# One block of a transformer on one core: the lower part of every fourth piece of split weights is made by ScalarE and an adding DMA instead of VectorE

## The chip, the core and the metric

The kernel runs on one core of a Trainium2 chip. The core has TensorE (PE, matrix products), VectorE (DVE), ScalarE (ACT), GpSimd (POOL) and SyncE (SP), an on-chip memory of 128 partitions, PSUM banks in which products add up, and 16 DMA engines that all queues share. The metric is the device time of one execution in microseconds (us), the median of the runs shown.

## What is computed

A block for 256 tokens of width 2048: a feed-forward part, a mixing part (eight heads of retention and eight of sparse attention, whose 64 keys for each query are chosen by an index score), and a second feed-forward part, each behind a norm and added to x, then a last norm. All in float32.

```python
x = x + 0.5 * swiglu(rmsnorm(x, ffn1_norm[l]), ffn1_w_gate[l], ffn1_w_up[l], ffn1_w_down[l])
h = rmsnorm(x, mix_norm[l])
proj = h @ w_in[l]
...
x = x + jnp.concatenate([ro, ao], axis=-1) @ w_out[l]
x = x + 0.5 * swiglu(rmsnorm(x, ffn2_norm[l]), ffn2_w_gate[l], ffn2_w_up[l], ffn2_w_down[l])
return rmsnorm(x, final_norm)
```

Nearly all of the work is in the products with the weights: gate and up (2048 x 5632 each) and down (5632 x 2048), twice, w_in (2048 x 6480) and w_out (2048 x 2048).

## The kernel before

**Products in two parts.** TensorE takes float32r, a float32 with fewer bits. To keep the accuracy, each weight W is split into hi, the rounded W, and lo = W - hi, and the activations likewise. A product is hi times both parts of the activations (512 columns: 256 tokens of each part, line 137) plus lo times the upper part (256 columns, lines 136 and 139). Where tokens stand still and the weights move (the values, lines 154 to 156) there are three products.

**Pieces and loads.** The weights are a stream of 686 pieces, counted here from 0. A usual piece is four k tiles (128 rows of a weight each) by 256 columns, 128 x 1024 numbers on chip. A load brings two pieces, 1 MB, into a tile raw of which there are three. A chunk of 256 columns of gate, up or a projection has four pieces; a chunk of a down projection has six, the last of them half as wide. A step of the program is the work beside the products of one piece: before the products of piece i, `split` is written for piece i+4, and other work (evacuation, silu, rotation, scores, softmax, retention) is put at fixed steps by `after`.

**Splitting.** `split` (line 204) first issues loads on SP's queue until two more than the piece's own are under way. A load waits for its raw tile, that is for the splits of the two pieces that lay there. Then ACT makes hi by a copy that rounds, and DVE makes lo by a subtraction. hi and lo have five buffers each (BUFS), so piece i+5 can be split when the products of piece i are done.

**Order.** Each engine runs its instructions in the order in which the program writes them; a semaphore is waited for where one reads or overwrites what another made. POOL has little to do: four masks of the scores (`causal`, line 603), and the loads of the constants, the positions (line 412), decay and qdec (lines 676 and 678, `ret_consts`), the last two needed by the retention (`ret_s`, line 700).

Of the kernel before, what the change touches and what calls it, by code (L numbers as in the profile page):

```python
# [19 lines left out]
P = 128  # L20
T = 256          # tokens
D = 2048         # model width
KT = D // P      # 16
FF = 5632
NCH = FF // 256  # 22 chunks of 256 hidden columns
HCH = NCH // 2   # 11 chunks in each half
HKT = 2 * HCH    # 22 k tiles in each half
NH = 8           # retention heads, attention heads
NI = 16          # index heads
TOPK = 64  # L30
EPS = 1e-6
FIRST_SQ = 4     # the step of the first squares of x
BUFS = 5         # split pieces of weights on chip
NEG = -3.0e38    # marks a score that is out or already taken
BIG = -1.0e30    # added to the logits of keys that are not attended
W_AV = 256 + NI
C_TWO_PI = 2.0 * math.pi
C1 = 6.28125                       # 2 pi in parts whose products with n < 2**16 are exact
C2 = round((C_TWO_PI - C1) * 2**17) / 2**17
# [6 lines left out]
def layer(ctx: ExitStack, tc: tile.TileContext, a: dict, out: bass.AP):  # L46
# [23 lines left out]

# [1 line left out]
    gains = new(one, [P, 4 * KT + NH], F32, "gains")  # L72
# [3 lines left out]

# [1 line left out]
    loads = []   # lists of (offset, source)  # L78
    pieces = []  # dict(load, off, n, mm); a step is the work beside one piece's products
    raws, split_of = {}, {}  # L80
    ends = {}    # step -> functions

    def after(step, fn):
        ends.setdefault(step, []).append(fn)

    # a function may be a generator of stages; it yields the steps from one stage to the next
    chains = []
# [13 lines left out]
    class Chunk:  # L101
        """Where the products of a chunk of columns add up: a bank for each block of 128."""
        acc = None
# [9 lines left out]
    class LastChunk:  # L113
        """The same, with the first block complete before the last piece's products for the second"""

# [7 lines left out]
    def mm_cols(chunk, blocks, kts, rhs, first, last):  # L123
        """W[k, 128 cols] stationary; the split activations [k, hi | lo] move."""

        def go(hi, lo):
            order = [(i, b) for i in range(len(kts)) for b in range(blocks)]
            if last and isinstance(chunk, LastChunk):
                order.sort(key=lambda ib: ib[1])
            for i, b in order:  # L130
                acc = chunk.bank(b)
                r = rhs(kts[i])
                st, sp = first and i == 0, last and i == len(kts) - 1
                c = (i * blocks + b) * P
                if sp:
                    TE.matmul(acc[:, T:], lhsT=lo[:, c:c + P], rhs=r[:, :T], start=False, stop=False)  # L136
                TE.matmul(acc, lhsT=hi[:, c:c + P], rhs=r, start=st, stop=sp)  # L137
                if not sp:
                    TE.matmul(acc[:, T:], lhsT=lo[:, c:c + P], rhs=r[:, :T], start=False, stop=False)  # L139

        return go

    def mm_rows(chunk, n, kts, rhs, first, last):
        """Tokens stationary; W[k, n cols] moves."""

# [14 lines left out]
    def block(src, l0, l1, width):  # L160
        """k tiles l0 to l1 of a chunk, which lie in DRAM as one block"""
        return src[P * l0 * width:P * l1 * width].rearrange("(p n) -> p n", p=P)

    def stream(src, kts, width, per_load, per_piece, rhs, chunk, maker, arg):
        """One chunk of columns over all its k tiles."""
        n = len(kts)
        for l0 in range(0, n, per_load):
            l1 = min(n, l0 + per_load)
            loads.append([(0, block(src, l0, l1, width))])
            for k0 in range(l0, l1, per_piece):  # L170
                k1 = min(l1, k0 + per_piece)
                pieces.append(dict(load=len(loads) - 1, off=(k0 - l0) * width, n=(k1 - k0) * width,
                                   mm=maker(chunk, arg, kts[k0:k1], rhs, k0 == 0, k1 == n)))
        return len(pieces)   # the step after the chunk's last

    def stream_pair(srcs, rhs, chunks):
        """The first two chunks side by side, while x is loaded."""
        for k0 in range(0, KT, 4):
# [25 lines left out]
    def split(i):  # L204
# [9 lines left out]
        S.activation(hi[:, :p["n"]], raw, AF.Copy)  # L214
        V.tensor_tensor(lo[:, :p["n"]], raw, hi[:, :p["n"]].bitcast(F32), op=OP.subtract)  # L215
        split_of[i] = (hi, lo)

# [1 line left out]
    s2 = {}  # L219

    def split_x(c, norm):
        """x * gain of two k tiles, split, for the next projections."""
        t = new(one, [P, 2, 512], F32R, f"xg{c}")
# [19 lines left out]
    def rsqrt(o, v, n):  # L243
        """o = v ** -0.5"""
        q = new(tmp, [P, 2 * NH], F32, "rs_q", 1)[:, :n]
# [6 lines left out]
    def act_table(fn):  # L252
        """An early use of fn, for the table that a later one needs."""
        t = new(tmp, [P, 1], F32, "table", 1)
# [4 lines left out]
    def row_of(tok):  # L259
        """[tokens, 2] -> [128, tokens], the same row in each partition, in PSUM"""  # L260
        diag = new(tmp, [P, 2, P], F32, "diag", 1)
# [8 lines left out]
    def add_squares(ps, sq, first, last):  # L270
        """Sums over the partitions of sq, a column for each token tile, in a bank of its own"""
        for t in range(2):
# [22 lines left out]

# [1 line left out]
    def ffn(which, norm, next_norm, last):  # L297
# [76 lines left out]
    def finish(chunk):  # L374
        """The last two k tiles of x, and the final norm."""
        c = KT // 2 - 1
# [15 lines left out]

# [1 line left out]
    nc.scalar.dma_start(gains, a["gains"])  # L394
# [11 lines left out]

    # cos and sin: [cos, sin] of the 128 wide heads, then of the index heads
    rot = new(one, [P, 4, T], F32, "rot")

    def tables():  # L410
# [23 lines left out]
        yield 1  # L434
        # what the rounding of n left outside of [-pi, pi]
        V.tensor_scalar(n, ang, 1.0 / C_TWO_PI, MAGIC, op0=OP.mult, op1=OP.add)
# [12 lines left out]

    # ================= the program =================  # L450
    def first_squares():
# [8 lines left out]

# [1 line left out]
    m0 = len(pieces)  # L462
# [8 lines left out]

    heads = {}   # name -> tiles of four blocks [128, 4, 256]
    done_at = {}
# [39 lines left out]
    cols("iq", a["w_iq"], 4, True)  # L513
    # index keys, in both halves of the partitions
    ikT = new(one, [P, 1, T], F32, "ikT")
    chunk_ik = Chunk()
    end = stream(a["w_ik"], list(range(KT)), 128, 16, 8, rhs_x, chunk_ik, mm_cols, 1)
    after(end, lambda: rope(chunk_ik, 1, ikT, True))
    # attention values and index weights, by token
    avw = new(one, [P, 2, W_AV], F32, "avw")  # L520
# [50 lines left out]

    # -- index scores, one query tile each --
    score = [new(one, [P, P], F32, "score0"), new(one, [P, T], F32, "score1")]

    def index_scores(t, h0, n):
        """n heads from h0 of query tile t: score += w * relu(q . k). Heads of the two halves of
        the partitions take different row tiles of the array, and different banks."""
        w = P if t == 0 else T
# [36 lines left out]
    def bias(t):  # L615
        """0 where a key was taken, BIG elsewhere"""
        V.tensor_scalar(score[t], score[t], NEG, BIG, op0=OP.not_equal, op1=OP.mult)
        causal(score[t], t, BIG)

# [50 lines left out]

    # -- retention --
    ret = {}
# [86 lines left out]

    # when  # L760
    s = m_av + 1
# [18 lines left out]
    for i in range(2):  # L780
        after(s + i, lambda i=i: k_tok(4 * i))
    for g in range(2):   # heads 0-3, 4-7
        h0 = 4 * g
# [33 lines left out]

# [1 line left out]
    n = len(pieces)  # L819
    n_split = 0  # L820
    for i in range(n):
        # the first pieces wait for their loads: work that is ready should not queue behind them
        ahead = 2 if i < 11 else BUFS - 1
# [11 lines left out]
def _constants():  # L835
    f = np.float32
    lg = np.log1p(-np.exp2(-5.0 - np.arange(NH, dtype=np.float64)))
    j = np.arange(P, dtype=np.float64)
    diff = j[None, :] - j[:, None]                                   # [key j, query i]
    decay = np.where(diff >= 0, np.exp(np.maximum(diff, 0.0)[:, None, :] * lg[None, :, None]).transpose(1, 0, 2),  # L840
                     0.0).transpose(1, 0, 2) * 128.0 ** -0.5          # [key j, head, query i]
    qdec = np.exp((j + 1)[None, :] * lg[:, None])                    # [head, query i]
    kdec = np.exp((P - 1 - j)[:, None] * lg[None, :]) * 128.0 ** -0.5
# [10 lines left out]
def _tiles(w, cols, per_load=8):  # L854
    """[k, n] -> [chunk of cols, k * cols]: what one load brings is one block [128, k tile * cols]"""
    k, n = w.shape
# [45 lines left out]
```

## Time and profile before

| what | value |
| --- | --- |
| median of 2 runs | 1932.65 us (1932.54 to 1932.77) |
| the profiled execution, from the first to the last instruction | 1931.7 us |
| busy: PE, DVE, ACT, POOL | 1914.8, 1207.8, 924.9, 5.3 us |
| moved by DMA | 356.44 MB |
| share of the 16 DMA engines taken by the weights' queue | 53.5% |

The profiled execution's own time is its span of 1931.7 us; the timed median lies 0.95 us above. Busy time is the time in which an engine runs an instruction; waiting and issuing DMAs are not in it. The chain is the series of instructions and waits that ended last, followed back from the end. A wait is put down to what came last.

### The profile page before, as it was taken

To read this page: it belongs to the slowest core of one execution; us is meant where nothing else is said; L and a number is where in the kernel's file an instruction comes from. 1 tells how busy PE (TensorE), PEld (TensorE's weight loads), DVE (VectorE), ACT (ScalarE), POOL (GpSimd) and SP (SyncE) were. 2 spreads that over 40 slices of the span, in tenths; PEclk is the share of its full clock that TensorE was granted. 3 is DMA by queue.
4 is the path that set the end of the run, shared out by engine and by line. 5 is a ranking of instruction groups with operands and counts; after the bars stand their busy time and mean duration, and the time that the engine had idled before them with its cause. 6 is when DMAs were issued, how large, how long until landed. Compare 5 with 4: busy or idle time off the path is not lost.

```text
span 1931.7 us, 26692 instructions
## 1 busy us (share of the span) xinstructions
PE 1914.8 (99%) x10936; PEld 1672.2 (87%) x10936; DVE 1207.8 (63%) x1444; ACT 924.9 (48%) x1127; POOL 5.3 (0%) x14
## 2 busy tenths in 40 slices
PE   8999999999999999999999999999999999999997
PEld 7888888888888888988888888888888888888886
DVE  7675655555656666688755766565655556655554
ACT  7444443344444445656544555444443344444442
POOL 0000000000000000000000000000000000000000
PEclk9999999999999999999999999999999999999999
DMA  7555555555555555545544555555555555555552
GB/s 287 187 184 196 178 178 189 197 192 182 194 182 184 180 188 202 177 156 196 175 153 158 187 179 191 182 194 182 189 180 182 194 188 193 187 184 191 179 181 104
DMA packets 53050, 356.44 MB, mean 185 GB/s; under 512 B 6048, under 2 KB 6048, under 8 KB 14144
## 3 DMA queue, kind: packets, MB, share of 16 engines
q1 hardware_dynamic: 52416, 353.52, 53.5%
q8 instruction: 85, 1.39, 0.3%
q0 software_dynamic: 368, 1.19, 0.2%
q14 instruction: 37, 0.30, 0.0%
q10 hardware_dynamic: 144, 0.04, 0.0%
HBM read 352.63 MB, written 2.10 MB: 184 GB/s over the span
## 4 chain that ended last, share of the span: by engine, by line
PE 99%; DVE 0%; DMA 0%; ACT 0%; issue 0%; DVEq 0%
PE acc L137 62%; PE acc L139 30%; PE acc L136 2%; PE acc L155 1%; PE acc L156 1%; PE acc L154 1%; PE sm L137 1%; PE sm L583 0%; PE sm L631 0%; PE sm L139 0%; DVE x L390 0%; DMA gains<-in_gains 0%; PE sm L724 0%; PE sm L700 0%; PE sm L662 0%; PE sm L267 0%
## 5 line engine op out<-in xcount | busy, mean ns | idle before, releaser
L137 PE MATMUL acc<-xg,hi 128*128 128x512 f32 x3504 | 1230.2, 395 | 5.8 <-DVE xg L227 5.8
L215 DVE TENSOR_TENSOR lo<-raw,hi 128x1024 fp32r<-128x1024 f32 (+2 forms) x686 | 817.2, 1194 | 665.9 <-ACT hi L214 664.2
L214 ACT ACTIVATE hi<-raw 128x1024 fp32r<-128x1024 f32 (+2 forms) x686 | 705.8, 1033 | 795.3 <-PE acc L137 754.2
L139 PE MATMUL acc<-xg,lo 128*128 128x256 f32 x3285 | 929.7, 283 | 0.0
L137 PEld LDWEIGHTS acc<-xg,hi 128*128 128x128 f32 x3504 | 652.6, 188 | 149.3 <-ACT hi L214 5.8
L139 PEld LDWEIGHTS acc<-xg,lo 128*128 128x128 f32 x3285 | 618.9, 188 | 5.0 <-DVE lo L215 0.4
L137 PE MATMUL acc<-mid,hi 128*128 128x512 f32 x1620 | 569.0, 398 | 0.0
L139 PE MATMUL acc<-mid,lo 128*128 128x256 f32 x1542 | 433.0, 281 | 0.0
L137 PEld LDWEIGHTS acc<-mid,hi 128*128 128x128 f32 x1620 | 302.0, 188 | 71.0 <-DVE mid L757 0.2
L139 PEld LDWEIGHTS acc<-mid,lo 128*128 128x128 f32 x1542 | 291.3, 189 | 1.6
L325 ACT ACTIVATE s<-e 128x512 f32<-128x512 f32 x44 | 27.8, 632 | 82.1 <-DVE e L323 82.1
L136 PE MATMUL acc<-xg,lo 128*128 128x256 f32 x219 | 61.1, 279 | 0.0
L317 DVE TENSOR_TENSOR e<-acc,b 128x512 f32<-128x512 f32 x88 | 60.1, 683 | 0.0
L315 ACT ACTIVATE b<-acc 128x512 f32<-128x512 f32 x88 | 51.1, 581 | 3.2 <-PE acc L137 3.2
L136 PEld LDWEIGHTS acc<-xg,lo 128*128 128x128 f32 x219 | 41.2, 188 | 5.0
L226 ACT ACTIVATE xg<-x,gains 128x256 fp32r<-128x256 f32 x48 | 21.5, 500 | 41.8 <-DVE x L808 19.5
L490 ACT ACTIVATE b<-e 64x512 f32<-64x512 f32 (+2 forms) x46 | 28.1, 612 | 15.6 <-DVE e L480 15.0
L154 PE MATMUL acc<-hi,xg 128*128 128x512 f32 (+1 forms) x96 | 34.9, 364 | 0.0
L155 PE MATMUL acc<-lo,xg 128*128 128x512 f32 (+1 forms) x96 | 34.5, 359 | 0.0
L156 PE MATMUL acc<-hi,xg 128*128 128x512 f32 (+1 forms) x96 | 34.5, 359 | 0.0
L331 DVE TENSOR_TENSOR e<-e,s 128x512 f32<-128x512 f32 x44 | 30.4, 692 | 1.5
L335 DVE TENSOR_TENSOR mid<-e,mid 128x512 fp32r<-128x512 f32 x44 | 30.1, 685 | 0.0
(149 smaller groups left out, 661.0 us busy)
## 6 DMA issues: line engine op xcount, KB each, us to landing
raw<-in_wgu SPq DMA_DIRECT2D x172, 1024.0 KB, 4.8
raw<-in_wd SPq DMA_DIRECT2D x64, 1024.0 KB, 4.8
raw<-in_wd SPq DMA_DIRECT2D x32, 768.0 KB, 4.2
raw<-in_w_out SPq DMA_DIRECT2D x16, 1024.0 KB, 4.8
raw<-in_w_iq SPq DMA_DIRECT2D x8, 1024.0 KB, 4.8
raw<-in_w_aq SPq DMA_DIRECT2D x8, 1024.0 KB, 4.8
raw<-in_w_rk SPq DMA_DIRECT2D x8, 1024.0 KB, 4.9
raw<-in_w_rq SPq DMA_DIRECT2D x8, 1024.0 KB, 4.9
```

The lines of the kernel that those rows point to most:

```text
L136: TE.matmul(acc[:, T:], lhsT=lo[:, c:c + P], rhs=r[:, :T], start=False, stop=False)
L137: TE.matmul(acc, lhsT=hi[:, c:c + P], rhs=r, start=st, stop=sp)
L139: TE.matmul(acc[:, T:], lhsT=lo[:, c:c + P], rhs=r[:, :T], start=False, stop=False)
L154: TE.matmul(o, lhsT=h, rhs=hi[:, i * n:(i + 1) * n], start=st, stop=False)
L155: TE.matmul(o, lhsT=h, rhs=lo[:, i * n:(i + 1) * n], start=False, stop=False)
L156: TE.matmul(o, lhsT=l, rhs=hi[:, i * n:(i + 1) * n], start=False, stop=sp)
L214: S.activation(hi[:, :p["n"]], raw, AF.Copy)
L215: V.tensor_tensor(lo[:, :p["n"]], raw, hi[:, :p["n"]].bitcast(F32), op=OP.subtract)
L315: S.activation(b, acc[:, :, T:], AF.Copy)
L317: V.tensor_tensor(g, acc[:, :, :T], b, op=OP.add)
L331: V.tensor_tensor(u, u, sil[c], op=OP.mult)
L335: V.tensor_tensor(h[:, :, T:], u, h[:, :, :T].bitcast(F32), op=OP.subtract)
```

## The change

Of every fourth piece after piece 11 (`i % 4 == 2`), lo is no longer hi subtracted from raw on DVE. ACT reads raw a second time and writes its negative, rounded, into lo: that is -hi. Then a DMA of POOL's queue reads raw and adds it onto lo on chip, so that lo = raw - hi. The other pieces are as before. These are the changed lines; the rest of the diff takes away comments only, so lines behind it move by four (the subtraction of line 215 is 219 after, 315 is 319, 603 is 607, 676 is 680).

```diff
         S.activation(hi[:, :p["n"]], raw, AF.Copy)
-        V.tensor_tensor(lo[:, :p["n"]], raw, hi[:, :p["n"]].bitcast(F32), op=OP.subtract)
+        if i % 4 == 2 and i > 11:
+            S.activation(lo[:, :p["n"]], raw, AF.Copy, scale=-1.0)
+            G.dma_start(lo[:, :p["n"]], raw, accum_op=OP.add)
+        else:
+            V.tensor_tensor(lo[:, :p["n"]], raw, hi[:, :p["n"]].bitcast(F32), op=OP.subtract)
         split_of[i] = (hi, lo)
```

ACT's order around the split of piece 178, in the first feed-forward part, before (hi, raw and lo are the tiles of the split; b is an evacuated half of a chunk, s its silu):

```order
L214 ACTIVATE hi_4120<-raw_4024 128x1024
L315 ACTIVATE b_4124<-acc_4034 128x512
L214 ACTIVATE hi_4145<-raw_4024 128x1024
L325 ACTIVATE s_4150<-e_4126 128x512
L214 ACTIVATE hi_4170<-raw_4073 128x1024
L214 ACTIVATE hi_4190<-raw_4073 128x1024
```

And the same place of ACT after the change:

```order
L214 ACTIVATE hi_4161<-raw_4064 128x1024
L216 ACTIVATE lo_4162<-raw_4064 128x1024
L319 ACTIVATE b_4166<-acc_4075 128x512
L214 ACTIVATE hi_4187<-raw_4064 128x1024
L329 ACTIVATE s_4192<-e_4168 128x512
L214 ACTIVATE hi_4212<-raw_4114 128x1024
L214 ACTIVATE hi_4232<-raw_4114 128x1024
```

The pass that makes the negative stands right behind the hi pass of its piece, ahead of the evacuation b.

POOL's order in the mixing part before (score tiles are the index scores of the two query tiles; decay and qdec go into tiles named mid):

```order
L603 AFFINE_SELECT score_17_99<-score_17_99 128x128 x2
L603 AFFINE_SELECT score_18_100<-score_18_100 128x256 x2
L676 DMA mid_7993<-in_decay 128x1024
L678 DMA mid_7995<-in_qdec 128x1024
L897 UNCONDITIONAL_BRANCH
```

And the same place of POOL after the change, from the first mask on; the DMAs into lo are the adds of pieces 310, 314, 318, 322, 326, 330 and 334:

```order
L607 AFFINE_SELECT score_17_99<-score_17_99 128x128
L217 DMA lo_7303<-raw_7165 128x1024
L607 AFFINE_SELECT score_17_99<-score_17_99 128x128
L217 DMA lo_7443<-raw_7300 128x1024
L607 AFFINE_SELECT score_18_100<-score_18_100 128x256
L217 DMA lo_7549<-raw_7440 128x1024
L607 AFFINE_SELECT score_18_100<-score_18_100 128x256
L217 DMA lo_7661<-raw_7546 128x1024
L217 DMA lo_7765<-raw_7658 128x1024
L217 DMA lo_7879<-raw_7762 128x1024
L217 DMA lo_7987<-raw_7876 128x1024
L680 DMA mid_8074<-in_decay 128x1024
```

The adds now stand between the masks, and decay's load behind the adds of pieces 326, 330 and 334.

## Rows read from the trace of the kernel before

**Rows 1.** The page: busy us, share of the span, instructions of each engine.

```profile
PE 1914.8 (99%) x10936; PEld 1672.2 (87%) x10936; DVE 1207.8 (63%) x1444; ACT 924.9 (48%) x1127; POOL 5.3 (0%) x14
```

**Rows 2.** The page: the chain that ended last, its shares by engine.

```profile
PE 99%; DVE 0%; DMA 0%; ACT 0%; issue 0%; DVEq 0%
```

**Rows 3.** Waits: who waited for whom; us in total, times, longest us.

```profile
ACT hi L214 <- PE acc L137: 754.2, 520, 2.9
...
PEld acc L137 <- ACT hi L214: 5.8, 1, 5.8
```

**Rows 4.** Waits of SP's DMA queue; us in total, times, longest us.

```profile
SPq L202 <- DVE lo L215: 1648.9, 320, 8.9
```

**Rows 5.** Groups by shape: count, then busy us, mean ns, idle before.

```profile
L215 DVE TENSOR_TENSOR lo<-raw,hi 128x1024 fp32r<-128x1024 f32 x644 | 787.2, 1225 | 656.4 <-ACT hi L214 654.9 <-PE acc L137 0.3
L214 ACT ACTIVATE hi<-raw 128x1024 fp32r<-128x1024 f32 x644 | 679.5, 1058 | 763.0 <-PE acc L137 722.5 <-PE acc L156 29.0 <-issue 5.4
```

**Rows 6.** The chain in order of time: start us, us, what.

```profile
54.60 0.47 PE acc L137 x2
65.83 0.46 PE acc L137 x2
...
963.79 0.89 PE sm L700 x8
```

**Rows 7.** Timelines of ACT and PE, piece 150: start us, us, instruction.

```profile
403.59 1.06 ACT L214 ACTIVATE hi<-raw 128x1024 fp32r<-128x1024 f32 x1 [1.84 <-PE acc L137]
...
414.80 0.28 PE L139 MATMUL acc<-xg,lo 128*128 128x256 f32 x1
```

**Rows 8.** The same timelines, piece 98, in a down projection.

```profile
268.25 1.06 ACT L214 ACTIVATE hi<-raw 128x1024 fp32r<-128x1024 f32 x1 [1.75 <-PE acc L137]
...
278.15 0.28 PE L139 MATMUL acc<-mid,lo 128*128 128x256 f32 x1
```

**Rows 9.** The same timelines, piece 298, in the mixing part.

```profile
809.18 2.24 ACT L214 ACTIVATE hi<-raw 128x1024 fp32r<-128x1024 f32 x2
...
815.65 0.28 PE L139 MATMUL acc<-xg,lo 128*128 128x256 f32 x1
```

**Rows 10.** DMA queues (packets, MB, share) and issues (count, KB, us to landing).

```profile
q1 hardware_dynamic: 52416, 353.52, 53.5%
...
raw<-in_wgu SPq DMA_DIRECT2D x172, 1024.0 KB, 4.8
...
mid<-in_decay POOLq DMA_DIRECT2D x1, 512.0 KB, 4.8
mid<-in_qdec POOLq DMA_DIRECT2D x1, 512.0 KB, 8.9
```

**Rows 11.** Busy time by window: engines, granted clock, DMA share, GB/s.

```profile
884.00:888.00 4.00, 4.00 (x27) 3.56 (x26) 3.79 (x5) 2.39 (x4) 2.24 (x3) 1.00 0.83 280
```

**Rows 12.** Timeline of POOL, and PE's first use of lo of piece 322.

```profile
863.01 0.40 POOL L603 TENSOR_SCALAR_AFFINE_SELECT score<-score 128x256 f32<-128x256 f32 x1 [3.31 <-DVE score L598]
883.88 1.32 POOL L603 TENSOR_SCALAR_AFFINE_SELECT score<-score 128x256 f32<-128x256 f32 x1 [20.46 <-DVE score L617]
885.15 0.56 POOL L676 DMA_DIRECT2D mid<-in_decay  x1
885.70 0.53 POOL L678 DMA_DIRECT2D mid<-in_qdec  x1
...
891.44 0.28 PE L139 MATMUL acc<-xg,lo 128*128 128x256 f32 x1
```

**Rows 13.** Timeline of DVE beside these instructions of POOL.

```profile
883.72 1.22 DVE L215 TENSOR_TENSOR lo<-raw,hi 128x1024 fp32r<-128x1024 f32 x1
...
885.46 1.22 DVE L215 TENSOR_TENSOR lo<-raw,hi 128x1024 fp32r<-128x1024 f32 x1
```

## The prediction

> **What bounds the kernel now.** I read the shares of busy time first, then the chain that ended last, then the waits, then ACT and DVE beside TensorE in a steady stretch. TensorE is busy for 1914.8 of the 1931.7 us span and the chain lies on it for 99% [rows 1, 2]; the granted clock is 1.00 in the stretch of [rows 11], the upper of its two levels, 2.4 GHz. A chunk of four pieces (a piece is four k tiles of 256 columns) starts every 11.23 us, at 54.60 and 65.83 [rows 6], so a piece costs 2.81 us of TensorE and nothing else sets that pace. The list of waits says the same from the other side: ACT waits 754.2 us for TensorE to give a hi buffer back, and TensorE's weight load waits for ACT once, 5.8 us at the start [rows 3]. So the splits run ahead by as many pieces as there are buffers, and the question is only whether the new way of making lo comes within that lead. It can't make TensorE faster: no matmul goes or changes.
>
> **How much lead there is.** Pieces are counted from 0. The changed pieces are 14, 18, ... 682, 168 of 686, each the first piece of its load. Split i+5 waits for piece i to end, so split i begins four pieces before its products: 4 x 2.81 = 11.2 us. Piece 150 shows it: ACT starts hi at 403.59 and ends it 1.06 us later, TensorE takes lo at 414.80 [rows 7]. After a second ACT pass of 1.06 us [rows 5] there is **room** of 414.80 - 403.59 - 2.12 = 9.1 us for the adding DMA, from its issue to its landing. I did this sum for all 168 pieces (hi's end from ACT's rows, the first use of lo from TensorE's rows counted off in the program's order): 133 have 8.5 us or more, with a median of 9.1; 35 have less, 33 of them about 7.8, because a half piece (512 columns) of a down projection lies in their lead, as in piece 98: 278.15 - 268.25 - 2.12 = 7.8 [rows 8]. Two are tighter: 7.3 for piece 314, and 4.35 for piece 298, whose hi is made late (809.18, the first of two passes in that row) and whose lo is taken at 815.65: 815.65 - 809.18 - 2.12 = 4.35 [rows 9].
>
> **The change part by part.** *DVE* loses 168 passes of 1.225 us [rows 5], 206 us of 1207.8. It is never waited for in the steady state, so this is worth nothing. *ACT* gains 168 passes; with a scale they should last as the hi pass does, 1.058 us: 178 us, 924.9 becomes some 1103, 57% of the span. In a window of 11.2 us ACT then has five passes (5.3 us) and two or three small ones of 0.6 us; the evacuation behind the new pass starts up to 1.06 us later and its bank is wanted a whole chunk later. No cost; the pass itself is already in the room.
>
> *The adding DMA* is the unknown: no row shows one. Its bytes: 512 KB of raw and 512 KB of lo read, 512 KB written. The nearest row is the load of decay, 512 KB on the same POOL queue beside a weight load: 4.8 us from issue to landing [rows 10], in a stretch where the DMA engines were 83% busy [rows 11]. A second read at the rate of the weight stream adds 0.524 MB x (53.5% x 1931.7 us / 353.5 MB) = 1.5 us [rows 10]. I take **6.3 us**. The low end is 4.8 (the second read hidden). The high end is the other 512 KB load of that queue, qdec, which stood behind decay and beside weight loads and took 8.9 [rows 10], plus 1.5: 10.4 us. I stay near decay, because an add comes once in 11.2 us and has no neighbour on its own queue, while qdec had one 0.55 us ahead of it.
>
> Against the rooms, 6.3 us costs 6.3 - 4.35 = 1.9 us at piece 298 and nothing elsewhere. 4.8 costs 0.4. A late add gives the next one that much more room, since both leads hold the stall; so of adds that are late all through, every second one pays. With that, 7.8 us costs 4 us in total, 8.9 us 24 us, 9.5 us 57 us, 10.4 us 127 us (by hand: 133 x (10.4 - 9.1) + 35 x (10.4 - 7.8), halved, is 132).
>
> The Trainium skill (DMA: Bandwidth & Descriptors, "Anatomy of one DMA") gives 2.0 us plus bytes at 436 GB/s for a DMA of POOL. For 1 MB read that is an estimate of 4.4 us, and the sum would be 1931.7 + 0.1; the decay row, 4.8 for half of it, is dearer, and I keep the row.
>
> *The raw buffer* is now held by the add too. A load is issued when its second piece is split, 2.81 + 1.06 + 1.22 = 5.1 us after its first piece's split began; with the add it is 2.12 + 6.3 = 8.4. SP waits here for DVE's lo now, 320 times [rows 4]. The load lands 4.8 us later [rows 10], at 13.2, and its first split is wanted six pieces after, at 16.9: 3.7 us spare, and behind that stands the lead of the splits. What waits behind it on SP is only the next load. Cost 0.
>
> *The DMA engines* are 53.5% used by the weights [rows 10]. 168 adds are 88 MB, 13.3% for each time those bytes pass at the weights' rate; with two reads 27%, together 80%. That lengthens some weight loads, within the spare above.
>
> *POOL's queue.* Each add waits on POOL for ACT's pass; four masks of the scores, the loads of the positions, decay and qdec stand in the same queue. The mask that starts at 883.88 and takes 1.32 us [rows 12] now stands ahead of the add of piece 322, whose lo TensorE wants at 891.44 [rows 12]: 6.2 us are left, about what the add takes, and DVE comes to the mask earlier because it has fewer passes. The positions slide behind the add of piece 26, to some 2 us after piece 21 ends; they are a quarter of decay's bytes, so 4.8 us is ample, and they are read in the step of piece 27, after piece 26 ends at the earliest, 14 us on. Decay and qdec slide behind three more adds, 3 x 11.2 = 34 us, from 885 to 919; the products that need decay run at 963.79 [rows 6]. Cost 0 for all.
>
> Does DVE hold the issue up? In the row of 883.88 the mask, which reads on-chip memory, took 1.32 us beside DVE's pass of 883.72, against 0.40 for the same shape at 863.01 [rows 12, 13]. The two DMA issues of POOL that followed, 0.56 and 0.53 us, were no longer while DVE ran the next lo pass from 885.46 [rows 12, 13]. So a POOL instruction that reads can be held by DVE, an issue was not; if it were held for a whole pass, 6.3 becomes 7.5 and the sum grows by 1 to 2 us.
>
> The Trainium skill speaks against the change here (SBUF — State Buffer, the note on "DVE blocks DMA"): POOL can't write descriptors while DVE runs in a mode with two ports. It also says that a pass over two tensors has no such mode, and the two issue rows agree; by the harsher reading the sum would be the 1 to 2 us just given.
>
> **Sum.** The profiled execution: 1931.7 + 1.9 = 1933.6 us of span. The median of the timed runs lies 0.95 us over that span (1932.65), so the forecast is **1934.5 us**, no change.
>
> **The rivals.** *The add is late* (slower). If issue to landing takes more than about 9.2 us, TensorE waits at the lo matmul of every second changed piece, in the whole program. From the table above: 9.5 us gives 1990, 10.4 gives 2060. For it: qdec's 8.9, and that an add on the DMA engines has no row; against it: decay's 4.8 with the engines near full. It passes 2% (39 us) at some 9.2 us. Chance 0.18.
>
> *The DMA engines fill up* (slower). An add may cost the engines more than its two reads. They have 46.5% free; at 3.5 times a plain pass (3.5 x 13.3 = 46.5) they are full, and then the weights come late everywhere. At 4 times the demand is 106.7%: 1931.7 x 1.067 = 2061 us. For it: no row of an add; against it: it needs 3.5 passes where I count two. Chance 0.10.
>
> *DVE's relief helps TensorE* (faster). All of TensorE's idle time after the start is 16.9 - 5.8 = 11 us [rows 1, 3], nearly all of it the start-up's and the final norm's, so even the whole would give 1922, not 2%. A gain beyond needs matmuls faster than 2.81 us a piece, for which no row speaks. Chance 0.01.
>
> *The change doesn't do what it says*: adds gather in POOL's queue behind a mask that waits for DVE and do nothing but that. It is one place, 1 or 2 us: 1936, within the forecast. Chance 0.02.
>
> **How the numbers follow.** The forecast has 0.69, with the last rival 0.71 for within 2%; slower 0.18 + 0.10 = 0.28; faster 0.01. Two per cent is about what a measurement of this kernel can tell from no change. The range starts at 1930, as nothing can be gained, and goes to 2060, the price of the high end of the add; that holds the forecast and over half of the first rival, some 0.8.
>
> **What would show it.** Right: TensorE still 99% busy, chunks of 11.23 us, the adds landing in 5 to 8 us, hardly a wait of TensorE for a DMA into lo, ACT near 1100 us and DVE near 1000, DMA share near 80%. Wrong: a row of waits "PE for DMA lo", 84 or more times, with adds of 9 us and more; or a DMA share of 95% and more, with ACT's hi waiting for raw. Then the term at fault is the 6.3 us, or the second read as the add's only price on the engines.

## The result, and the profile after

The changed kernel takes 1992.47 us (1990.94 to 1994.0, two runs) against 1932.65: 1.0308 times the time before, interval 1.0288 to 1.0327. It is 3.1% slower. The forecast was no change, 1934.5 us; the time lies inside the range, at the place where the rival *The add is late* put it.

The page of the changed kernel answers to [rows 1, 2, 10]: busy time, the two large DMA queues (packets, MB, share), the chain's shares by engine and by line, the group of the adds' issues (busy us, mean ns, idle before), and the DMA issues with their median time to landing.

```profile
PE 1932.6 (97%) x10936; PEld 1669.0 (84%) x10936; DVE 1017.4 (51%) x1276; ACT 1084.1 (54%) x1295; POOL 147.7 (7%) x182
...
q1 hardware_dynamic: 52416, 353.52, 53.8%
q0 software_dynamic: 24560, 89.17, 22.7%
...
PE 62%; DMA 29%; issue 7%; DVE 1%; ACT 1%; SPq 0%; POOLq 0%; DVEq 0%; ACTq 0%
...
L217 POOL DMA_DIRECT2D lo<-raw x168 | 143.0, 851 | 1791.8 <-ACT lo L216 1732.6
...
raw<-in_wgu SPq DMA_DIRECT2D x172, 1024.0 KB, 5.9
lo<-raw POOLq DMA_DIRECT2D x167, 512.0 KB, 9.2
```

Start with the chain. It lay on TensorE for 99% [rows 2] and now lies on DMA for 29%. The engines do about what the prediction said (ACT 1084 us, DVE 1017, the two queues 76.5% of the DMA engines). The median add takes 9.2 us from issue to landing where 6.3 was taken, and the weights' loads take 5.9 where they took 4.8 [rows 10].

The waits of the changed kernel (us in total, times, longest), in two answers, all engines and SP's queue; they answer to [rows 3, 4]:

```profile
ACT hi L214 <- PE acc L137: 626.4, 496, 2.7
PEld acc L139 <- DMA lo<-raw: 69.9, 73, 2.6
PE acc L139 <- DMA lo<-raw: 42.1, 55, 2.1
ACT hi L214 <- DMA raw<-in_wgu: 38.2, 19, 2.9
ACT hi L214 <- DMA raw<-in_wd: 34.1, 19, 3.5
```

```profile
SPq L202 <- DMA lo<-raw: 1615.2, 167, 11.9
SPq L202 <- DVE lo L219: 146.5, 59, 7.2
```

TensorE stops 55 times for a lo that an add has not finished, 42.1 us in all. (The row of PEld counts the same stops from the weight load's side, and short ones that no matmul feels.) ACT waits 72 us for raw in these two rows, where it waited 0.6 us in all before the change. And SP, which waited 320 times for DVE, now waits 167 times for an add and only 59 times for DVE: of two loads, one waits for the add and the other stands behind it.

The chain in order of time (start us, us, what) shows the rhythm of the loss:

```profile
68.22 9.28 DMA lo<-raw
...
91.22 9.84 DMA lo<-raw
...
114.76 9.18 DMA lo<-raw
```

Most adds are issued 10 to 13 us apart, but one in 23 us is on the chain: every second one, as the prediction's halving had it. That doesn't hold all through, though. Here is the busy time by stretch of the changed kernel (us, busy us of the five engines with their instructions, granted clock, DMA share, GB/s):

```profile
45.00:780.00 735.00, 712.69 (x4006) 611.78 (x4005) 355.25 (x403) 382.86 (x435) 55.88 (x66) 1.00 0.80 225
780.00:1480.00 700.00, 697.18 (x4010) 608.19 (x4009) 404.66 (x558) 414.84 (x524) 53.01 (x65) 1.00 0.74 223
1480.00:1960.00 480.00, 462.65 (x2600) 397.12 (x2599) 211.40 (x229) 246.20 (x276) 35.73 (x42) 1.00 0.79 223
```

TensorE is idle for 22.3, 2.8 and 17.4 us of them. And the adds' time from issue to landing in nearly the same stretches (the line of the adds at 45 to 790, 800 to 1474 and 1480 to 1960 us; the first row, of the whole run, is the issue's own duration in ns, min/median/max):

```profile
L217 POOL DMA_DIRECT2D lo<-raw x168: 837/854/877, 35.0 to 1960.2; - x168
...
DMA to landing us min/median/max: 7.3/9.3/10.6
...
DMA to landing us min/median/max: 4.1/5.2/9.3
...
DMA to landing us min/median/max: 7.3/9.4/10.6
```

The same add, of the same size, takes 9.3 us in one stretch and 5.2 in another, and the second stretch holds gate and up of the first half of the last feed-forward part, whose code is that of the first part: there the median is 6.0 us, in the first part 9.3. So the add has no fixed price. What differs is when the loads go. The timelines of SP, POOL and TensorE at 417 us, in a stretch of late adds (start us, us, instruction; x2 means two issues with no gap):

```profile
417.61 0.80 SPq L202 DMA_DIRECT2D raw<-in_wgu  x2
419.90 0.85 POOL L217 DMA_DIRECT2D lo<-raw  x1 [10.46 <-ACT lo L216]
429.87 0.39 PE L139 MATMUL acc<-xg,lo 128*128 128x256 f32 x1 [0.75 <-DMA lo<-raw]
429.88 0.80 SPq L202 DMA_DIRECT2D raw<-in_wgu  x2
431.96 0.85 POOL L217 DMA_DIRECT2D lo<-raw  x1 [11.21 <-ACT lo L216]
```

And SP and POOL at 1191 us, in the stretch of quick adds:

```profile
1191.53 0.85 POOL L217 DMA_DIRECT2D lo<-raw  x1 [10.45 <-ACT lo L216]
1196.39 0.33 SPq L202 DMA_DIRECT2D raw<-in_wgu  x1
1199.94 0.33 SPq L202 DMA_DIRECT2D raw<-in_wgu  x1
1202.83 0.85 POOL L217 DMA_DIRECT2D lo<-raw  x1 [10.45 <-ACT lo L216]
```

In the **spread rhythm** (1191 us) the add lands after 4.8 us and lets one load go at 1196.39; the other load goes at 1199.94, when its own tile comes free, 2.9 us ahead of the next add. In the **paired rhythm** (417 us) the add lands after 9.9 us, later than that second load could have gone; SP's queue is in order, so both loads go at 429.88, in 0.8 us, and the next add is issued 2.1 us behind them. It lands late, and so on.

By the trace's packet records, the add issued at 419.90 moves its first packet at 424.9, when 237 of the 256 packets of the two loads have started: 5.0 us after its issue (the median of all adds is 4.5). Where an add has no load ahead of it (experiment 2, below), the first packet follows 1.4 to 1.5 us after the issue. For the 167 adds after 45 us I set the time of each against the landing of the last load that was issued before it (counted from the records of the trace):

| last load lands, us after the add's issue | adds | median of the add, issue to landing |
| --- | --- | --- |
| 0 to 2 | 24 | 4.6 us |
| 2 to 4 | 28 | 5.4 us |
| 4 to 6 | 16 | 7.7 us |
| 6 to 8 | 44 | 9.2 us |
| over 8 | 55 | 9.5 us |

So an add ends behind the loads that stand ahead of it. This is an association; the experiments below test which way it works.

**The 60.5 us of span, added up.** The 55 stops are 42.1 us. A stop costs more than its idle time: at 428.72 a matmul that no other follows lasts its full 0.40 us instead of giving way after 0.23, and the first one behind the stop, at 429.87, gives way after 0.22 instead of 0.12; together 0.27 us, 55 times 14.9 us (an estimate from this one stop), and this is counted as busy. With 1.4 us of a slower clock (last section) it is 58.4 of 1992.2 - 1931.7 = 60.5. TensorE's busy time says much the same: it grew by 17.8 us, from 1914.8 to 1932.6.

### The profile page after: what moved, and what is told of

Read it like the earlier page. It is cut to its first block, busy times and chain, and to the rows that moved or that the text cites. A ratio compares the mean times of both kernels' runs of the same rounds, so it can differ in the third digit from the quotient of the medians.

```text
span 1992.2 us, 27235 instructions
## 1 busy us (share of the span) xinstructions
PE 1932.6 (97%) x10936; PEld 1669.0 (84%) x10936; DVE 1017.4 (51%) x1276; ACT 1084.1 (54%) x1295; POOL 147.7 (7%) x182
## 3 DMA queue, kind: packets, MB, share of 16 engines
q0 software_dynamic: 24560, 89.17, 22.7%
## 4 chain that ended last, share of the span: by engine, by line
PE 62%; DMA 29%; issue 7%; DVE 1%; ACT 1%; SPq 0%; POOLq 0%; DVEq 0%; ACTq 0%
PE acc L137 37%; DMA lo<-raw 21%; PE acc L139 19%; DMA raw<-in_wd 6%; DMA raw<-in_wgu 1%; PE acc L136 1%; PE acc L154 1%; PE acc L155 1%; PE acc L156 1%; ACT hi L214 1%; DVE lo L219 1%; PE sm L137 0%; PE sm L587 0%; PE sm L635 0%; PE sm L139 0%
## 5 line engine op out<-in xcount | busy, mean ns | idle before, releaser
L219 DVE TENSOR_TENSOR lo<-raw,hi 128x1024 fp32r<-128x1024 f32 (+2 forms) x518 | 613.2, 1185 | 604.8 <-ACT hi L214 603.3
L217 POOL DMA_DIRECT2D lo<-raw x168 | 143.0, 851 | 1791.8 <-ACT lo L216 1732.6
L216 ACT ACTIVATE lo<-raw 128x1024 fp32r<-128x1024 f32 x168 | 175.1, 1042 | 0.0
L231 DVE SCALAR_TENSOR_TENSOR xg<-x,gains,xg 128x256 fp32r<-128x256 f32 x48 | 20.9, 482 | 20.1 <-ACT xg L230 20.1
```

The source lines that it names most:

```text
L216: S.activation(lo[:, :p["n"]], raw, AF.Copy, scale=-1.0)
L217: G.dma_start(lo[:, :p["n"]], raw, accum_op=OP.add)
```

## The experiments

Three theories stood at the start. **The slow add** (S): an add on chip takes 9 us by itself. **The full engines** (F): loads and adds together fill the DMA engines, so everything takes longer. **The loop of adds and loads** (L): the add holds its raw tile, SP's queue waits for its landing, the loads then go in pairs, and the pair stands ahead of the next add. Where an expectation speaks of two states, it means the two rhythms above. All edits are made to the changed kernel; the kernel before took 1933.0 to 1933.1 us on the same chips, and each ratio is against it.

**1. The ACT pass alone.** No add; DVE makes lo again, after ACT's pass.

```diff
             S.activation(lo[:, :p["n"]], raw, AF.Copy, scale=-1.0)
-            G.dma_start(lo[:, :p["n"]], raw, accum_op=OP.add)
+            V.tensor_tensor(lo[:, :p["n"]], raw, hi[:, :p["n"]].bitcast(F32), op=OP.subtract)
```

> ACT's second pass stays, the adding DMA is left out and DVE makes lo of these pieces again, over ACT's result. Theory L (loop): the add by itself takes 4 to 5 us; it takes 9.2 because it holds its raw tile, SP's load waits for that, two loads then go out back to back, and the next add's packets stand behind theirs. Theory S (slow add): an add of this size on POOL's queue takes 9 us whatever else moves. Theory F (full engines): the DMA engines are too full at 77%. All three put the loss on the DMA: 1931 to 1935 us, no wait of TensorE for lo. If the pass on ACT is part of the loss, 1940 or more.

1933.94 us, 1.0004 (0.9994 to 1.0013). The pass on ACT costs nothing; all of the loss belongs to the add.

**2. The add without the loads.** The loads of weights behind the eighth are left out, and the pieces are split from what lies in the raw tiles.

```diff
     def load(i):
+        if i >= 8:
+            raws[i] = raws[5 + i % 3]
+            return
         raws[i] = new(wts, [P, 2048], F32, "raw", 3)
```

> The loads after the eighth are left out; later pieces split what loads 5 to 7 brought, so the adds run alone on the DMA engines. L and F: adds of 4 to 5 us from issue to landing, no wait of TensorE for lo, 1930 to 1935 us. S: adds of 9 us, TensorE waits as before, 1980 to 1993 us.

1934.03 us, 1.0005 (0.9995 to 1.0014). From the page of this run, the queue of the loads and the adds:

```profile
q1 hardware_dynamic: 4320, 12.58, 1.8%
...
lo<-raw POOLq DMA_DIRECT2D x167, 512.0 KB, 4.5
```

An add with the engines to itself takes 4.5 us, less than the low end of the prediction. The slow add falls. The Trainium skill (DMA: Bandwidth & Descriptors, "Anatomy of one DMA") gave an estimate of 4.4 us if the bytes of both reads are counted; the run agrees with it.

**3. The same add, not holding raw.** It reads a tile of zeros on chip instead of raw, so lo is -hi; loads, adds and bytes stay (one mid tile fewer makes the room).

```diff
+    fixed = new(one, [P, 1024], F32, "fixed")
+    after(5, lambda: V.memset(fixed, 0.0))
...
-            G.dma_start(lo[:, :p["n"]], raw, accum_op=OP.add)
+            G.dma_start(lo[:, :p["n"]], fixed[:, :p["n"]], accum_op=OP.add)
```

> The add reads a tile of zeros that stays on chip instead of raw (so lo of these pieces is only minus hi; two tiles of another pool are given up for one of zeros). Bytes and packets of the adds are the same, but raw is no longer held by them. L: SP issues a load every 5.6 us as before the change, adds of 5 to 7 us, TensorE hardly waits for lo, 1931 to 1940 us. S: adds of 9 us, 1980 to 1993. F: DMA share still 75% or more with adds of 9 us and 1980 to 1993.

1939.09 us (1936.12 to 1939.43), 1.0027 (1.0016 to 1.0038). The page, then SP's and POOL's timelines at the same place as above:

```profile
q1 hardware_dynamic: 52416, 353.52, 51.8%
q0 software_dynamic: 24560, 89.17, 25.0%
...
lo<-fixed POOLq DMA_DIRECT2D x167, 512.0 KB, 4.8
```

```profile
418.18 0.33 SPq L204 DMA_DIRECT2D raw<-in_wgu  x1
421.06 0.85 POOL L219 DMA_DIRECT2D lo<-fixed  x1 [10.38 <-ACT lo L218]
423.81 0.33 SPq L204 DMA_DIRECT2D raw<-in_wgu  x1
429.43 0.33 SPq L204 DMA_DIRECT2D raw<-in_wgu  x1
```

The queues take 76.8% of the engines, as in the changed kernel, and the adds take 4.8 us. So the engines are not full; F falls. The loads go one by one, 5.6 us apart. What has gone is the hold on raw, and with it nine tenths of the loss. Of what is left, two early adds (10.7 us from 34.36, 9.2 from 94.43, the chain's longest) stop TensorE; I did not follow them further.

**4. A plain copy.** The DMA copies raw into lo without adding, so lo is raw; it holds raw as the add does.

```diff
-            G.dma_start(lo[:, :p["n"]], raw, accum_op=OP.add)
+            G.dma_start(lo[:, :p["n"]], raw)
```

> The DMA copies raw into lo without adding (lo of these pieces is then raw itself): one read instead of two. L: 3.5 to 5.5 us from issue to landing, so a load is held back by less than 1 us and no two go out together; 1931 to 1936 us. S, if it is POOL's queue that is slow: 8 us and more, 1970 or more; S, if it is the adding that is slow: 4 to 5 us and 1931 to 1936, as L. F: DMA share near 66%, 1931 to 1940.

1933.72 us, 1.0003 (0.9993 to 1.0012). It lands in 3.5 us and takes 13.3% of the engines. SP waits for it 167 times (1030.6 us) and hardly a pair forms: after 45 us one load was issued within 1 us of the load before it, against 109 in the changed kernel. Holding raw does no harm by itself; it does when the DMA that holds it can end behind the time at which the second load would go.

**5. and 6. More buffers.** Six of hi and lo (5), or four raw tiles (6); each with 14 mid tiles.

```diff
-BUFS = 5
+BUFS = 6
```

> Six hi and lo buffers instead of five (two tiles of another pool are given up for them), so splits lead by one more piece, 2.8 us. L: adds still land in 9 us, since raw is held as before, but the room is 11.9 us, so TensorE does not wait for lo. If the lead was all that was short: 1933 to 1940 us. If the weights' own loop (raw landed, split, add, next load, three loads in 16.9 us) is short too: ACT waits for raw and 1945 to 1975.

```diff
-        raws[i] = new(wts, [P, 2048], F32, "raw", 3)
+        raws[i] = new(wts, [P, 2048], F32, "raw", 4)
```

> Four raw tiles instead of three (two tiles of another pool are given up), five hi and lo buffers. Loads still go out when an add has landed, so the pairs stay. L: adds of 9 us, TensorE waits for lo as after the change, 1980 to 1993 us, but ACT no longer waits for raw. If the late loads were the cause, 1933 to 1945.

Six buffers: 1970.57 us (1963.69 to 1975.4), 1.0191 (1.0164 to 1.0219). Four raw tiles: 1980.67 us (1969.99 to 1989.45), 1.0244 (1.0204 to 1.0284). The adds take 9.4 and 9.1 us. The waits that stand out, with six buffers and then with four raw tiles:

```profile
ACT hi L214 <- DMA raw<-in_wgu: 209.1, 97, 6.3
ACT hi L214 <- DMA raw<-in_wd: 199.8, 74, 5.3
```

```profile
PE acc L139 <- DMA lo<-raw: 39.7, 50, 2.4
```

Neither ends the loss. More lead for lo makes ACT wait for raw (TensorE still stops 33 times for lo, 31.1 us); more raw takes ACT's wait away and leaves TensorE's. So two limits lie close together: the lead of the splits, and the round of the raw tiles.

**7. Half as many adds.** Every eighth piece.

```diff
-        if i % 4 == 2 and i > 11:
+        if i % 8 == 2 and i > 11:
```

> Every eighth piece instead of every fourth, 84 adds of the same size. L: the pair of loads that an add brings about has passed when the next add is issued, 22.5 us later, so an add meets single loads: 4.8 to 6.5 us, hardly a wait of TensorE, 1932 to 1937 us. If an add is late whatever came before it, 9 us and 1940 to 1965.

1934.40 us, 1.0006 (0.9997 to 1.0016); the 84 adds take 4.7 us and the chain is back at TensorE for 99%. With four loads between two adds hardly a pair forms: after 45 us three loads follow another within 1 us.

**8. An add that nobody waits for.** ACT's pass and the add go into a spare tile; DVE makes lo as before (14 mid tiles).

```diff
         if i % 4 == 2 and i > 11:
+            lo = new(wts, [P, 1024], F32R, "lx", 2)
             S.activation(lo[:, :p["n"]], raw, AF.Copy, scale=-1.0)
             G.dma_start(lo[:, :p["n"]], raw, accum_op=OP.add)
+            lo = new(wts, [P, 1024], F32R, "lo", BUFS)
+            V.tensor_tensor(lo[:, :p["n"]], raw, hi[:, :p["n"]].bitcast(F32), op=OP.subtract)
```

> The pass of ACT and the add go into a spare tile that nothing reads, and DVE makes lo of these pieces as before the change (two tiles of another pool are given up), so TensorE never waits for an add, but raw is held by it. L: loads go out in pairs and adds land in 8 to 10 us as after the change, without TensorE waiting for lo; 1932 to 1945 us, more only if ACT waits for raw.

1962.03 us, 1.0147 (1.0132 to 1.0162): much more than expected (the expectation allowed it only if ACT waits for raw, and ACT does). TensorE never waits for an add here. ACT's waits for raw in the whole run, then the chain in order of time, in the first down projection:

```profile
ACT hi L213 <- DMA raw<-in_wgu: 188.9, 88, 4.3
ACT hi L213 <- DMA raw<-in_wd: 177.0, 65, 6.6
```

```profile
291.38 10.38 DMA lx<-raw
...
302.23 7.12 DMA raw<-in_wd
...
311.76 10.35 DMA lx<-raw
...
322.58 8.56 DMA raw<-in_wd
```

This chain has no TensorE in it. It is the round of the raw tiles: the add lands, SP issues two loads, the second lands 7 to 8.6 us later, its first piece is the next but one to get an add, and that add starts 20.4 us behind the first. Eight pieces of a down projection take TensorE about 8 x 5.5/6 x 2.81 = 20.6 us (every sixth piece is a half one). So the round of the raw tiles alone fills the time, and where it is longer, ACT waits for raw. That makes a loss half as large as the changed kernel's without any late lo. How it reaches TensorE is argued, not shown: TensorE's idle time grew by 16.5 us and its busy time by 8.8, and the longest new stops (5.14 us at 775.3, 2.69 at 647.5) were waits for other work of DVE. What two mid tiles fewer cost by themselves was not run, here and in 5 and 6; no wait for products that still read a mid tile stands in these lists.

**9. An add of half the width.** ACT and the add make the first half of the columns, DVE the other.

```diff
+            n2 = p["n"] // 2
-            S.activation(lo[:, :p["n"]], raw, AF.Copy, scale=-1.0)
-            G.dma_start(lo[:, :p["n"]], raw, accum_op=OP.add)
+            S.activation(lo[:, :n2], raw[:, :n2], AF.Copy, scale=-1.0)
+            G.dma_start(lo[:, :n2], raw[:, :n2], accum_op=OP.add)
+            V.tensor_tensor(lo[:, n2:p["n"]], raw[:, n2:], hi[:, n2:p["n"]].bitcast(F32), op=OP.subtract)
```

> Of the same pieces, only the first half of the columns is made by ACT and the add (256 KB), the other half by DVE as before. L: alone such an add lands in about 3.5 us, raw is free at about the time at which DVE's lo of the next piece frees it anyway, so no load is held back and no two go out together: adds of 3.3 to 5 us, 1932 to 1936 us. If any adding DMA in every fourth piece brings the late state: adds of 7 us and more, 1950 to 1985.

1933.53 us, 1.0002 (0.9993 to 1.0012); the adds take 3.7 us. As with the plain copy, SP waits for 167 of them (1017.0 us), and it does no harm.

**10. A late start.** The same adds from piece 42 on. The start-up, in which loads are split into parts and x is loaded between them, could be what makes the first pair.

```diff
-        if i % 4 == 2 and i > 11:
+        if i % 4 == 2 and i > 40:
```

> No add before piece 42 (first after the change: piece 14), so none while x and the first weights are being loaded. L with two states (an add that meets two loads is itself late and pairs the next two loads; one that meets a single load is not, and the state stays until something disturbs it): adds of 4.5 to 6 us from piece 42 to the first down projection (piece 88), where it turns; the 4.8 us that TensorE lost before piece 88 are gone, 1985 to 1989 us. Without memory (each add late because of the density of the loads in its stretch): adds of 9 us from the first on, 1988 to 1993.

1982.23 us (1979.59 to 1982.7), 1.0249 (1.0232 to 1.0266), a little under the 1985 to 1989 that were expected. The adds' landing at 112 to 280 us, and at 330 to 790:

```profile
DMA to landing us min/median/max: 4.5/4.8/5.6
...
DMA to landing us min/median/max: 7.9/9.4/10.4
```

Until 280 us the adds take 4.8 us; in the changed kernel the same pieces' adds took 9.2. The code of that stretch is the same in both, so it is what went before that sets the price. It turned in the first down projection, whose half pieces shorten the time between adds; that they are what turned it was not tried by itself.

**11. No adds in the down projections either.** 113 adds are left.

```diff
-        if i % 4 == 2 and i > 11:
+        if i % 4 == 2 and i > 40 and not (88 <= i < 136 or 224 <= i < 272 or 502 <= i < 550 or 638 <= i):
```

> As e10, and no adds in the four down projections (pieces 88 to 135, 224 to 271, 502 to 549, 638 to 685), where a half piece comes in every chunk. L with two states: nothing turns it, adds of 4.5 to 7.5 us in all gate, up and mixing stretches, 1932 to 1938 us. Without memory: the losses of the gate and up stretches stay, 1950 to 1965.

1939.11 us (1938.1 to 1950.64), 1.0045 (1.0022 to 1.0067); just missed. The adds start at 4.5 us again, but in the second stretch of gate and up they turn late with no down projection near. The records of the trace:

| add issued at | last load lands, us after | the add takes |
| --- | --- | --- |
| 461.33 | 2.1 | 4.6 us |
| 472.56 | 4.7 | 7.1 us |
| 483.79 | 5.1 | 7.5 us |
| 495.02 | 7.1 | 8.4 us |
| 506.25 | 5.9 | 8.6 us |
| 517.48 | 8.2 | 9.4 us |

Each add was issued 11.23 us after the one before it. One load, issued at 469.70, landed after 7.6 us where its neighbours took 4.8 to 5.0; the add behind it took 7.1, and from there the loop tightened by itself. Why that load was slow stays open. Four of the five runs lie at 1938.1 to 1942.6 us and one at 1950.6; only one was traced, so whether the rhythm turned at another place in that one isn't known.

**12. One add in eight left out.** If an add's price hung on its own place alone, an eighth of the adds would take an eighth of the loss with it; if the rhythm carries the price on, each gap resets it.

```diff
-        if i % 4 == 2 and i > 11:
+        if i % 4 == 2 and i > 11 and i % 32 != 30:
```

> Every eighth of the adds is left out (pieces 30, 62, 94, ... are split as before the change), 147 adds of 168. L with two states: a gap of 22 us lets the single loads come back, so each gap ends a late stretch, and what turns it again are the down projections; 1940 to 1970 us. Without memory: seven eighths of the loss, 1980 to 1988.

1944.93 us, 1.0061 (1.0046 to 1.0076). An eighth of the adds left out takes away four fifths of the loss: 11.9 us remain of 59.8. The wait of TensorE in this run:

```profile
PE acc L139 <- DMA lo<-raw: 9.1, 12, 1.8
```

TensorE's stops fall from 55 to 12, and the median add lands after 6.0 us instead of 9.2, so the price itself fell for the adds that stayed: those issued from 183 to 250 us, behind a gap, took 4.5 to 4.7 us, the three ahead of it 9.2 to 10.2. So the loop has memory, and L stands.

No version beats the kernel before: TensorE is busy for 1914 us or more in all of them, and the best with adds that make lo (7 and 9) only draw level.

## Why the prediction went wrong, point by point

- **TensorE is the bound, and relief of DVE is worth nothing: right.** DVE 1017 us (some 1000 expected), ACT 1084 (1103); the pass on ACT is free (experiment 1).
- **The add's price, 6.3 us: wrong, and not only in size.** Alone it takes 4.5 us, below the range's low end. In the changed kernel the median is 9.2, which lies near qdec's 8.9 [rows 10]. I set that row aside because an add "has no neighbour on its own queue". Its neighbours are on the other queue: qdec stood "beside weight loads", as the prediction itself says, and so does every add of a paired rhythm.
- **The raw buffer, "Cost 0": this is the step that failed.** The time for which the add holds raw was seen (8.4 us after the first split), and so was that the next load waits behind it on SP. I counted the spare of one load and did not ask what is late next: two loads that go together, 2 MB ahead of the next add. The sum took the add's price as given (6.3 us) and the loads' start as a result; each sets the other, and the price became 9.3. With the measured figures the spare of 3.7 us is gone as well. The first load of the pair at 429.88 lands after 5.5 us: 2.12 + 9.3 + 5.5 = 16.9, all of its room. The second, issued 0.4 us later, lands after 9.5: 2.12 + 9.3 + 0.4 + 9.5 = 21.3, where its first split is wanted eight pieces on, 22.5 us, or 20.6 in a down projection. Experiment 3 takes the hold away and leaves the loads, the adds and their bytes: nine tenths of the loss go. Experiment 8 keeps the hold and takes the wait for lo away: half as much is lost.
- **The rival "The add is late": the mechanism was right, and the time in part by luck.** TensorE waits at the lo matmul, every second add of the two stretches that lose pays (53 stops, 108 adds), and the room at the stops was about what the prediction took: at 419.90 the add took 9.9 us and TensorE stopped for 0.75. It gave 1990 us at 9.5; the adds take 9.3 to 9.4 there, and the time is 1992. But the rival had them late all through, and between 780 and 1480 us TensorE stopped only twice; what a stop costs beyond its idle time, which the rival lacked, made up for that: 42.1 us are idle time, 16.3 are not. The raw tiles' round hardly enters: at 46 of the 55 stops ACT had begun that piece's hi as soon as TensorE gave the buffer back, at one it had waited for raw. Its chance, 0.18, was too low because the only row for it, qdec, was read as an exception.
- **The rival "The DMA engines fill up": wrong.** 76.5% (80% estimated); the same share without loss in experiment 3.
- **POOL's queue and DVE's hold on POOL: right.** The 168 issues took 837 to 877 ns, with DVE busy for 51% of the span. The positions landed after 9.1 us where 4.8 was called ample, and nothing waited for them. In the mixing part, where the masks stand, TensorE loses least.

What is shown and what is argued: that the hold on raw is needed for the loss (3), that the loads are (2), that a shorter DMA escapes it (4, 9), and that the price is carried from add to add (10, 12). That the pair's packets go ahead of the add's is read from the packet records and the first table; no run changed the order in which the engines take the two queues, and none kept the hold but moved the loads out of one in-order queue, which would tell the pairs from the hold. What goes with it is the number of pairs: after 45 us a load follows another within 1 us 109 times in the changed kernel, 113 to 115 times in 5, 6 and 8, 89 in 10, 30 in 12, 20 in 11, and at most 3 in 1, 3, 4, 7 and 9. What turns the rhythm at a given place was seen only as an occasion (start-up, a down projection, one slow load), and what turns it back near 790 to 800 us, where two adds lie 14.5 us apart, was not tried.

## What to carry to other kernels

When a transfer starts to hold a buffer that another transfer waits for, don't price it as a constant: write both issue times down for two or three rounds, with the in-order queue between them, and see whether the waiting ones go in a bunch and stand ahead of the next. Near such a point a small thing decides: half the width or half the number is free and a gap in every eighth place costs 0.6%, while the full pattern loses 3%. One buffer more, on either side, did not end the loss.

## What the runs showed of the hardware

- **An add's packets began only behind loads that were already queued; after that both queues moved side by side.** The add of 419.90 was issued 2 us behind two loads of the other queue and moved nothing until 424.9; by experiment 2 it could have begun 3.5 us earlier, and in these 3.5 us the records show loads' packets alone. Then both run: the last packets start in turn (load 427.96, add 428.28, load 428.58, add 428.90), and of the two loads issued just ahead of the add of 329.22, 109 of 256 packets start between the add's first packet and its landing. The Trainium skill (DMA: Bandwidth & Descriptors, "Queues, rings and completion order") says that an engine goes round between the queues that have work, packet by packet. The trace agrees with that for the end of such an add; the 3.5 us ahead of its first packet it does not explain, unless nearly a whole load counts as one packet, which no run here shows.
- **An adding packet costs nearly twice a plain one.** A 4 KB packet takes 328 ns when it adds (changed kernel) and 174 ns in the plain copy of experiment 4; the queue's share is 22.7% against 13.3%. The issue on POOL takes 0.85 us against 0.53.
- **A stop of 2 us lowered TensorE's clock in one place and not in another.** Windows of the changed kernel, then TensorE's timeline there:

```profile
782.00:786.00 4.00, 1.87 (x11) 1.32 (x11) 2.79 (x4) 2.36 (x3) 0.00 (x0) 1.00 0.59 120
786.00:790.00 4.00, 4.00 (x15) 3.37 (x16) 1.74 (x4) 2.03 (x4) 0.85 (x1) 0.57 0.80 262
```

```profile
785.87 0.39 PE L139 MATMUL acc<-xg,lo 128*128 128x256 f32 x1 [2.13 <-DMA lo<-raw]
...
786.58 0.63 PE L137 MATMUL acc<-xg,hi 128*128 128x512 f32 x1
...
789.74 0.40 PE L137 MATMUL acc<-xg,hi 128*128 128x512 f32 x1
```

TensorE was busy for 1.87 of 4 us and stopped for 2.13 at the end of them; then its matmuls of 512 columns took 0.63 us instead of 0.40, at the lower level of 1.2 GHz, until 789.6. The five pairs of matmuls from 786.58 took 3.16 us instead of 5 x 0.35: 1.4 us lost. Stops of 0.75 us, as at 429.87, left the clock at 1.00. A stop of 1.79 us in experiment 12 (until 1485.25) lowered it as well, but one of 2.11 us in experiment 5 (until 837.08) did not, so the length of the stop alone doesn't decide it.
